# Moving the last chunk's Gram blocks into the first Gram group, with other weight columns and earlier left sums

## The chip, the cores and the metric

The kernel runs on one core of a Trainium2 chip. The metric is the device time of one execution, in microseconds (us). The kernel before takes 1006.29 us, the median of three runs (1004.66 to 1007.55). The changed kernel computes the same function.

## The reference

One layer of a hybrid network runs over 528 frames (16 meta frames and 512 real ones) of width 2048. What has to be computed is, cut to what matters:

```
hn = rmsnorm(h);  P = hn @ w_in                       # 528 x 2048 by 2048 x 8320
r, k, v, g, wl, al = token_shift(P[:, :4224])         # RWKV half: 16 heads of 64
decay = exp(-exp(-softplus(-(w0 + tanh(wl) @ W)) - .5));  a = sigmoid(a0 + al @ A)
kk = normalise(k * k_k);  k = k * (1 + (a - 1) * k_a)
S = S*diag(w) - (S kk)(kk*a)^T + v k^T;  y = S r      # one step per frame
y_a = (groupnorm(y) + bonus) * silu(g)
y_b = B * causal_conv3(C * h) * silu(gc)              # convolution half
out = rmsnorm(h + concat(y_a, y_b) @ w_out)[16:]      # 512 x 2048 by 2048 x 2048
```

## The kernel before, in words

**Precision.** Each large product is made of three products of a 32-bit format that TensorE takes at full pace: high times high, high times low, low times high. For that every operand is split into a high and a low part. Weights arrive by DMA in raw tiles; `split_w` (L134, L135) makes the high part on ACT and the low part on DVE or POOL, into one of six slots of 1152 columns (`slot`). `column(j)` says at which column of the slot the weights of a projection begin: 0, 16 or 80. The high part takes 512 columns from there, and the low part the 512 behind it.

**Projections.** The 65 blocks of 128 columns of w_in are taken in the order of `plan`: low-rank inputs (lora), then k, r, v, g of eight head pairs, mixed with C, h, B, gc of the convolution half. `main` runs one of them: for each of four groups of four k-tiles, `steps` (L328) issues 12 matmuls for each range of frames. k, v and lora have two ranges, of 256 and 272 frames; r, g, C and h of 256 and 258; B and gc one, of 512. For k the ranges are taken in the order (1, 0), for the others (0, 1). The results are in banks of PSUM from the pool `pm`, tag "main", which has four: a projection with two ranges holds two of them, the next one takes the other two. A bank is given back when the instructions that read it have run: `scaled` (L352) on DVE, one piece for the first range and, for k and v, three pieces for the second (256, 2 and 14 columns).

**One stream on TensorE.** TensorE's order is written out by hand. `flow` is a generator that issues one matmul of the projections at a time and charges 0.43 ns for each column; `fill(ns)` takes matmuls from it until their charges add up to `ns`. The recurrence's small steps stand between such fills, so that TensorE always has projection matmuls to do while another engine prepares the next small step. `FW` holds the lengths.

**Preparing a head pair.** `prepare(i)` makes, for head pair i, the decayed keys and queries, and then the Gram blocks of nine chunks of 64 frames. `gram` issues two products per chunk, each shown as two records (L681). First group: after a fill of `FW["gram"]` = 8000 (even pairs) or `FW["gram_b"]` = 13500 (odd pairs) come chunks 0 to 7, into two banks of `pz` (tag "tz") and two of `pi` (tags "misc" and "ser"); `masked` (L691) reads them on DVE, two instructions for each four chunks. After a further fill of `FW["gram2"]` = 5500 comes the second group: chunk 8 into two "tz" banks, the squared norms n2 in two halves (L713, L714; two matmuls each, the second half in the rest of a bank that chunk 8 uses), and zb (L716, L717). ACT copies n2 and zb, and DVE masks chunk 8. `invert`, `load_inverse` and `recur` work further with the results.

**Order on the other engines.** DVE, ACT, POOL and the DMA queues are put in order by a planner ahead of the run: it goes by the order in which the code emits the instructions, moved forward where `ahead()` says so (`masked` and the copies of n2), and takes what is ready by its own times. On the chip each engine then runs its queue strictly in that order.

**Output product.** It is a Strassen-like scheme with seven products per half (`units`: M1, M2, then P5, M7, M3 and Q6 in four groups, P4). `at(u, ...)` attaches work to unit u: splits of weights (`split_unit`, L1215 on ACT, L1216 on DVE), sums of weights (`add`, L1206), sums of the left operand (`sums`, L1118 and L1121 on DVE), their splits (`split_form`, L1173 on ACT, L1174 on DVE), and the closing of products (`onto`, L1224). The four sums of the left operand's second half stand at units 6, 7, 8 and 9.

Of the kernel before, what the change touches and what calls it, by code (L numbers as in the profile page):

```python
# [9 lines left out]
F32 = mybir.dt.float32  # L10
# [8 lines left out]
P = 128  # L19
# [6 lines left out]
NCH = SEQ // CH + 1  # L26
LP = NCH * CH
# [15 lines left out]
FW = dict(  # L43
    evac=34, start=1062, lora=2200, gram=8000, gram_b=13500, gram2=5500, misc=2000, v=2000, vt=1000, solve=24500, solve_first=30000,
    tr=3200, lev=3000, cp=4200, out=1500, begin=19500, p=2900, u=2900, s=5200, last=3700, mix=2600,
)
# [31 lines left out]
def hymba_kernel(ctx: ExitStack, tc: tile.TileContext, xt, xtok, front, w_in, w_out, pv, lup, cst, msk, gf, out):  # L78
# [35 lines left out]

    def column(j):
        what = plan[j][0]
        return {"B": 0, "gc": 0, "v": 80, "g": 80, "h": 80}.get(what, 16)
    stream += [w_out[0, g] for g in range(3)]
    quarters, chain, low = {}, {}, {}
    state = {"next": 0}  # L120
# [5 lines left out]
    def slot_of(q):  # L126
        if q >= 2 * N_IN:
            return slot(f"w{q}", OUT_AT)
        n = q // 2
        return slot(f"w{q}", column(n % 4 if n < 8 else n // 2))  # L130
# [7 lines left out]
    def prefetch(upto):  # L138
        while state["next"] < min(upto, len(stream) if chain else N_IN):
            j = state["next"]  # L140
            raw = chain[j - N_IN] if j >= N_IN else wp.tile([P, 1024], F32, tag="raw", name=f"wr{j}", bufs=3)
            state["dma"] = nc.sync.dma_start(raw, stream[j]).ins
            with tc.high_priority(offset=WEIGHTS):
                for q in range(2):
                    split_w(2 * j + q, raw[:, q * 512 : (q + 1) * 512], nc.gpsimd if q and 10 < j < N_IN else nc.vector)
            state["next"] = j + 1
# [19 lines left out]
    pm = ph1.enter_context(tc.tile_pool(name="pm", bufs=4, space=PSUM))  # L166
    pz = ph1.enter_context(tc.tile_pool(name="pz", bufs=2, space=PSUM))
    pi = ph1.enter_context(tc.tile_pool(name="pi", bufs=1, space=PSUM))
# [5 lines left out]
    def tr(name, dt=F32):  # L174
        return cq.tile([P, LP], dt, tag="tr", name=name, bufs=5)
# [143 lines left out]
    def steps(ps, ranges, k4, q, ks=range(4), rs_=range(2)):  # L319
        hi, lo = quarters[q]  # L320
        for r, (a, b) in enumerate(ranges):
            if r not in rs_:
                continue
            for k in ks:
                kt = 4 * k4 + k
                w = slice(k * P, (k + 1) * P)
                for n, (ww, xx) in enumerate(((hi, xh), (hi, xl), (lo, xh))):
                    nc.tensor.matmul(  # L328
                        ps[r], ww[:, w], xx[:, kt, a:b], start=(kt == 0 and n == 0), stop=(kt == KT - 1 and n == 2)
                    )  # L330
                    yield (b - a) * 0.43

    def banks(ranges, name, pool, tag):
        return [pool.tile([P, b - a], F32, tag=tag, name=f"ps_{name}_{r}") for r, (a, b) in enumerate(ranges)]

    def main(j, ranges, name):
        prefetch(2 * j + 4)
        ps = banks(ranges, name, pm, "main")
        for k4 in range(4):
            if k4 == 1:  # L340
                prefetch(2 * j + 5)
            for r in (1, 0) if name[0] == "k" else range(len(ranges)):
                yield from steps(ps, ranges, k4, 4 * j + k4, rs_=(r,))
        return ps

# [137 lines left out]
    def mains():  # L483
# [34 lines left out]
        for j in range(4, len(plan)):  # L518
            what, i = plan[j]
            rg = FULL if what in ("k", "v") else REAL if what in ("B", "gc") else TAIL  # L520
            ps = yield from main(j, rg, f"{what}{i}")
            if what == "B" and i < 4 or (what, i) == ("gc", 0):
                state["split"] = low[4 * j + 4]
            use(what, i, ps)
# [17 lines left out]
    def step():  # L542
        t = next(flow, None)
        if t is None:
            run_pending(float("inf"))
        else:
            clock[0] += t
            run_pending(clock[0])
        return t

    def fill(ns):
        while ns > 0:
            seen = len(ready)
            t = step()
            if t is None:
                return
            ns -= t
            if len(ready) > seen:
                ns += FW["evac"]
# [5 lines left out]
    def low_rank(i, j, up, w0, name, pad):  # L565
        t = tr(name)
        nc.gpsimd.memset(t[:, META:CH], pad)
        hi, lo = up
        for a, b in ((0, 272), (272, L)):
            z = pz.tile([P, b - a], F32, tag="tz", name=f"{name}_{a}")  # L570
            nc.tensor.matmul(z, hi[:, j], la[:, j, a:b], start=True, stop=False)
            nc.tensor.matmul(z, lo[:, j], la[:, j, a:b], start=False, stop=True)
            with tc.high_priority(offset=AHEAD):
                if a == 0:
                    nc.scalar.activation(t[:, 0:META], z[:, 0:META], AF.Tanh, bias=w0, scale=0.5)
                    nc.scalar.activation(t[:, CH : 5 * CH], z[:, META:272], AF.Tanh, bias=w0, scale=0.5)
                else:
                    nc.scalar.activation(t[:, 5 * CH : LP], z, AF.Tanh, bias=w0, scale=0.5)
            fill(FW["lora"])
        return t  # L580


    def ahead():
        return tc.high_priority(offset=AHEAD)
# [13 lines left out]
    def split(t, name, n):  # L598
        hi = tr(f"{name}_h", F32R)[:, 0:n]
        lo = tr(f"{name}_l", F32R)[:, 0:n]  # L600
        nc.scalar.copy(hi, t)
        nc.vector.tensor_tensor(out=lo, in0=t, in1=hi.bitcast(F32), op=ALU.subtract)
        return hi, lo
# [23 lines left out]
    def prepare(i):  # L627
        p = i % 2
        until("k", i)
        k = got["k", i]  # L630
# [6 lines left out]
        tz = low_rank(i, 0, up, hv[:, 0, i : i + 1], f"tz{i}", -1.0)  # L637
# [26 lines left out]
        r = got["r", i]  # L664
# [8 lines left out]
        nc.scalar.activation(sq, k, AF.Square, scale=col(V_KK, i))  # L673
        sqh, sql = split(sq, f"sq{i}", LP)
        rh, rl = split(r, f"rk{i}", SEQ)
        fill(FW["gram_b" if p else "gram"])

        gt = cq.tile([P, 2, NCH, P], F32, tag=f"gt{p}", name=f"gt{i}")
        def gram(z, c, c0):
            for h, hs, ho in heads:  # L680
                nc.tensor.matmul(  # L681
                    z[h][:, c - c0],
                    bk[hs, c, h : h + 2, :].rearrange("p a s -> p (a s)"),
                    ar[hs, c].rearrange("p a s -> p (a s)"),
                    start=True, stop=True,
                )

        def masked(z, c0, c1):
            with ahead():
                for h in range(2):  # L690
                    nc.vector.tensor_tensor(  # L691
                        out=gt[:, h, c0:c1],
                        in0=z[h],
                        in1=gmask[:, h].unsqueeze(1).to_broadcast([P, c1 - c0, P]),
                        op=ALU.mult,
                    )


        za = [pz.tile([P, 4, P], F32, tag="tz", name=f"g{i}_0_{h}") for h in range(2)]
        zc = [pi.tile([P, 4, P], F32, tag=("misc", "ser")[h], name=f"g{i}_4_{h}") for h in range(2)]  # L700
        for c in range(8):
            gram(za if c < 4 else zc, c, c // 4 * 4)
        masked(za, 0, 4)
        masked(zc, 4, 8)
        fill(FW["gram2"])

        ze = [pz.tile([P, P + 288 * (1 - h)], F32, tag="tz", name=f"g{i}_8_{h}") for h in range(2)]
        gram([z[:, 0:P].unsqueeze(1) for z in ze], 8, 8)
        n2 = tr(f"n2{i}")
        zn = pi.tile([2, 288], F32, tag="misc", name=f"n2_{i}")  # L710
        zs = ((zn, 0, 288), (ze[0][0:2, P : P + 288], 288, LP))
        for z, a, b in zs:
            nc.tensor.matmul(z, ones[:, P : P + 2], sqh[:, a:b], start=True, stop=False)  # L713
            nc.tensor.matmul(z, ones[:, P : P + 2], sql[:, a:b], start=False, stop=True)  # L714
# [3 lines left out]
        with ahead():  # L718
            for z, a, b in zs:
                nc.scalar.copy(n2[0:2, a:b], z)  # L720
            masked([z[:, 0:P].unsqueeze(1) for z in ze], 8, 9)
        nc.scalar.copy(r, zb)
        fill(FW["misc"])

# [90 lines left out]
        v = got["v", i]  # L815
# [246 lines left out]
    for i in range(0, NPAIR, 2):  # L1062
        invert([prepare(i), prepare(i + 1)])
# [155 lines left out]
    def here(t, n):  # L1219
        return xa[t][:, n * 512 : (n + 1) * 512] if n < 2 else xb[n - 2][:, t]  # L1220
# [61 lines left out]
    def at(u, fn, *args):  # L1282
        calls.setdefault(max(u, -1), []).append((fn, args))
# [67 lines left out]
                at(m2 - 2, split_unit, (0, "M2", g), passing(0, 1, 0, g))  # L1351
    for n, f in enumerate(("S1", "S3", "S4", "S5")):
        at((1, 2, 4, 5)[n], split_form, f, 0)
        at(6 + n, sums, 1, (n,))
        at((10, 11, 13, 14)[n], split_form, f, 1)
    for t in range(4):
        at((0, 1, 8, 9)[t], load_xa, t)
# [14 lines left out]
    z = {}  # L1372
    for u, unit in enumerate(units):
        half, prod, g = unit
# [53 lines left out]
    with tc.manual_schedule(engines={mybir.EngineType.DVE, mybir.EngineType.Activation, mybir.EngineType.Pool}):  # L1428
# [16 lines left out]
        for part in range(2):  # L1445
# [7 lines left out]
            h = here(1, 2)[:, cols]  # L1453
# [73 lines left out]
```

## Time and profile before

| | us |
|---|---|
| median of three runs | 1006.29 |
| the profiled execution's own time | 1006.95 |
| its span, first to last instruction | 1005.2 |
| PE busy in the span | 993.7 |
| DVE, ACT, POOL busy | 680.5, 393.2, 264.2 |

The span is the stretch that the trace covers; the time of an execution lies 1.75 us above it here. In rows of groups the columns are the line, the engine, the operation, the result and its operands, the shapes and the count, then the busy time in us and the mean duration of one in ns, then the idle time before them and what ended it. In rows of the timeline they are the start in us from the span's start, the length in us, the engine, the line and the operands, the count of instructions merged into the row, and idle time before it in brackets. Matmuls overlap in the pipeline: two that start 0.11 us apart each last 0.28 us. The pace is therefore read from differences of starts.

### The profile page before, as it was taken

What the parts mean: (1) busy time and instruction counts of PE and PEld (TensorE: products, weight loads), DVE (VectorE), ACT (ScalarE), POOL (GpSimd) and SP (SyncE); (2) the same over time, 40 slices, a digit from 0 to 9 for tenths busy, and PEclk for the clock granted to TensorE, in tenths of its full rate; (3) what the DMA queues carried; (4) which work ended last, traced back from release to release, by engine and by line L of the source; (5) the groups of instructions that cost most, each with busy time, mean ns of one, the idle gap of its engine ahead of it and who ended that gap; (6) DMA issues with size and microseconds to landing.
All of it is one profiled execution on the core that took longest, in us unless ns stands there. A gap on an engine that the chain in (4) does not pass through costs nothing.

```text
span 1005.2 us, 23750 instructions
## 1 busy us (share of the span) xinstructions
PE 993.7 (99%) x9723; PEld 913.6 (91%) x9723; DVE 680.5 (68%) x1313; ACT 393.2 (39%) x729; POOL 264.2 (26%) x286
## 2 busy tenths in 40 slices
PE   9999999999999999999999999999999999999996
PEld 8999998999998999998999998989888898788886
DVE  6777965587775568655668654245554597899996
ACT  7553422344323434323434322223232435545553
POOL 0122323224222323232423222223332333001001
PEclk9999999999999999999999999999999999999998
DMA  9525476446674363864273855978673689688644
GB/s 329 151 83 146 124 191 152 146 119 152 144 185 148 103 169 91 224 159 119 85 171 98 222 143 167 341 243 249 202 226 91 174 270 238 197 267 236 151 105 168
DMA packets 185181, 175.35 MB, mean 174 GB/s; under 512 B 121584, under 2 KB 142832, under 8 KB 184560
## 3 DMA queue, kind: packets, MB, share of 16 engines
q1 hardware_dynamic: 182480, 164.92, 56.4%
q0 software_dynamic: 2304, 8.39, 5.0%
q8 instruction: 76, 1.25, 0.5%
q10 hardware_dynamic: 288, 0.52, 0.1%
q14 instruction: 33, 0.27, 0.1%
HBM read 137.44 MB, written 36.35 MB: 173 GB/s over the span
## 4 chain that ended last, share of the span: by engine, by line
PE 65%; DVE 3%; DMA 1%; ACT 1%; SPq 0%; issue 0%; DVEq 0%; POOL 0%; ACTq 0%
PE ps_gc L328 8%; PE ps_B L328 7%; PE ps_h L328 7%; PE ps_C L328 6%; PE M L1243 5%; PE ps_k L328 5%; PE ps_v L328 5%; PE ps_g L328 5%; PE ps_r L328 5%; PE P L1243 4%; PE Q L1243 2%; PE zy L1010 1%; PE zs L1006 1%; PE g L681 1%; PE rz L954 1%; DVE o L1216 1%
## 5 line engine op out<-in xcount | busy, mean ns | idle before, releaser
L135 POOL TENSOR_TENSOR w<-wr,w 128x512 fp32r<-128x512 f32 x119 | 166.6, 1401 | 366.8 <-ACT w L134 306.2
L134 ACT CAST w<-wr 128x512 fp32r<-128x512 f32 x252 | 153.0, 618 | 280.7 <-PE ps_C L328 46.2
L135 DVE TENSOR_TENSOR w<-wr,w 128x512 fp32r<-128x512 f32 x133 | 95.8, 727 | 102.3 <-ACT w L134 92.2
L328 PE MATMUL ps_k<-xh,w 128*128 128x256 f32 (+1 forms) x512 | 95.8, 285 | 0.1
L328 PE MATMUL ps_r<-xh,w 128*128 128x256 f32 (+1 forms) x512 | 95.1, 281 | 0.0
L328 PE MATMUL ps_v<-xh,w 128*128 128x272 f32 (+1 forms) x512 | 95.0, 283 | 0.0
L328 PE MATMUL ps_h<-xh,w 128*128 128x258 f32 (+1 forms) x512 | 94.1, 282 | 0.0
L328 PE MATMUL ps_C<-xh,w 128*128 128x258 f32 (+1 forms) x512 | 93.2, 281 | 0.0
L328 PE MATMUL ps_g<-xh,w 128*128 128x258 f32 (+1 forms) x512 | 91.9, 281 | 0.0
L328 PE MATMUL ps_B<-xh,w 128*128 128x512 f32 x256 | 83.4, 395 | 0.1
L328 PE MATMUL ps_gc<-xh,w 128*128 128x512 f32 x256 | 81.7, 393 | 0.3 <-DVE w L135 0.3
L328 PEld LDWEIGHTS ps_h<-xh,w 128*128 128x128 f32 x512 | 79.7, 189 | 1.8 <-issue 1.2
L328 PEld LDWEIGHTS ps_k<-xh,w 128*128 128x128 f32 x512 | 80.4, 189 | 0.7 <-DVE w L135 0.3
L328 PEld LDWEIGHTS ps_r<-xh,w 128*128 128x128 f32 x512 | 80.3, 189 | 0.2
L328 PEld LDWEIGHTS ps_v<-xh,w 128*128 128x128 f32 x512 | 80.0, 189 | 0.3
L328 PEld LDWEIGHTS ps_C<-xh,w 128*128 128x128 f32 x512 | 79.7, 189 | 0.6
L328 PEld LDWEIGHTS ps_g<-xh,w 128*128 128x128 f32 x512 | 79.3, 189 | 0.3
L328 PE MATMUL ps_k<-xl,w 128*128 128x272 f32 (+1 forms) x256 | 72.9, 285 | 0.0
L328 PE MATMUL ps_v<-xl,w 128*128 128x256 f32 (+1 forms) x256 | 72.5, 283 | 0.0
L328 PE MATMUL ps_r<-xl,w 128*128 128x256 f32 (+1 forms) x256 | 72.4, 283 | 0.0
L328 PE MATMUL ps_g<-xl,w 128*128 128x256 f32 (+1 forms) x256 | 72.3, 282 | 0.0
L328 PE MATMUL ps_C<-xl,w 128*128 128x256 f32 (+1 forms) x256 | 72.0, 281 | 0.0
(320 smaller groups left out, 2261.9 us busy)
## 6 DMA issues: line engine op xcount, KB each, us to landing
wr<-in_w_in_dram SPq DMA_DIRECT2D x126, 512.0 KB
ct<-opd SPq DMA_DIRECT2D x64, 288.0 KB
wo<-in_w_out_dram SPq DMA_DIRECT2D x21, 512.0 KB
x<-in_w_out_dram POOLq DMA_DIRECT2D x16, 512.0 KB, 5.8
opd<-ar SPq DMA_DIRECT2D x8, 576.0 KB
opd<-gt SPq DMA_DIRECT2D x16, 288.0 KB
opd<-bt SPq DMA_DIRECT2D x64, 64.0 KB
x<-in_w_out_dram SPq DMA_DIRECT2D x8, 512.0 KB
```

Of the source, the lines that this page charges most:

```text
L134: nc.scalar.copy(hi, rq)
L135: low[q] = eng.tensor_tensor(out=lo, in0=rq, in1=hi.bitcast(F32), op=ALU.subtract).ins
L328: nc.tensor.matmul(ps[r], ww[:, w], xx[:, kt, a:b], start=(kt == 0 and n == 0), stop=(kt == KT - 1 and n == 2))
L681: nc.tensor.matmul(z[h][:, c - c0], bk[hs, c, h : h + 2, :].rearrange("p a s -> p (a s)"), ar[hs, c].rearrange("p a s -> p (a s)"), start= ...
L954: nc.tensor.matmul(z[e][ho if e else hs, 0, k], t[hs, o : o + CH], t[hs, O_V : O_V + CH] if part else st[hs, 4 * e + k], start=(part == 0 ...
L1006: nc.tensor.matmul(d[hs, j], w, x[hs], start=(a == 0), stop=(a == b - 1))
L1010: nc.tensor.matmul(d[ho, j], t[hs, o : o + CH], x[hs], start=(a == 0), stop=(a == b - 1))
L1216: nc.vector.tensor_tensor(out=lo, in0=rq, in1=hi.bitcast(F32), op=ALU.subtract)
L1243: nc.tensor.matmul(bank[s], left(prod, jj, m, s), w, start=(jj == 0 and n == 0), stop=(jj == 7 and n == 2))
```

## The change

There are three edits.

First, the columns: lora, k and r weights begin at column 80 of their slots instead of 16, as v, g and h do already; only C stays at 16, and B and gc at 0. The ranges of k are taken in the order (0, 1).

Second, the Gram blocks of chunk 8 are issued with chunks 0 to 7, into two banks of the projections' pool `pm`, and masked right behind the other masks. The fill ahead of the first group is longer by 2000 for pair 0 and by 2500 for pair 1, shorter by 4000 for pair 3; the fill behind it makes up for that, so that the second group stays where it was. In the second group n2 gets one bank of "misc" and one of "tz".

Third, the four left sums of the output stand at units 5, 5, 7 and 9.

```
     def column(j):
-        return {"B": 0, "gc": 0, "v": 80, "g": 80, "h": 80}.get(what, 16)
+        return {"B": 0, "gc": 0, "C": 16}.get(what, 80)
...
-            for r in (1, 0) if name[0] == "k" else range(len(ranges)):
+            for r in range(len(ranges)):
...
-        fill(FW["gram_b" if p else "gram"])
+        shift = {0: 2000, 1: 2500, 3: -4000}.get(i, 0)
+        fill(FW["gram_b" if p else "gram"] + shift)
...
-        for c in range(8):
-            gram(za if c < 4 else zc, c, c // 4 * 4)
+        ze = [pm.tile([P, 1, P], F32, tag="main", name=f"g{i}_8_{h}") for h in range(2)]
+        for c in range(NCH):
+            gram((za, zc, ze)[c // 4], c, c // 4 * 4)
         masked(za, 0, 4)
         masked(zc, 4, 8)
-        fill(FW["gram2"])
-
-        ze = [pz.tile([P, P + 288 * (1 - h)], F32, tag="tz", name=f"g{i}_8_{h}") for h in range(2)]
-        gram([z[:, 0:P].unsqueeze(1) for z in ze], 8, 8)
+        masked(ze, 8, 9)
+        fill(FW["gram2"] - shift)
+
         n2 = tr(f"n2{i}")
-        zn = pi.tile([2, 288], F32, tag="misc", name=f"n2_{i}")
-        zs = ((zn, 0, 288), (ze[0][0:2, P : P + 288], 288, LP))
+        zn = [pool.tile([2, 288], F32, tag=t, name=f"n2_{i}_{t}") for pool, t in ((pi, "misc"), (pz, "tz"))]
+        zs = ((zn[0], 0, 288), (zn[1], 288, LP))
...
-            masked([z[:, 0:P].unsqueeze(1) for z in ze], 8, 9)
...
-        at(6 + n, sums, 1, (n,))
+        at((5, 5, 7, 9)[n], sums, 1, (n,))
```

## The prediction

> **What bounds the kernel now.** I read the page's first part, then the waits of TensorE (PE), then its groups with shapes kept apart, and last the timeline of PE and DVE around the places that the edits touch. The first two say that PE is never short of work:
>
> ```profile
> span 1005.2 us, 23750 instructions
> PE 993.7 (99%) x9723; PEld 913.6 (91%) x9723; DVE 680.5 (68%) x1313; ACT 393.2 (39%) x729; POOL 264.2 (26%) x286
> ```
>
> ```profile
> PE M L1243 <- DVE o L1216: 0.6, 2, 0.4
> PE ps_gc L328 <- DVE w L135: 0.3, 1, 0.3
> ```
>
> The second fence is from the waits of PE (total us, times, longest): its waits for other engines are below a microsecond each. So an edit gains only if PE streams fewer or faster instructions, and it loses whatever wait it puts into PE's row. Both are worked out below against the profiled execution, whose span is 1005.2 us and whose time is 1006.95, that is 0.66 above the median 1006.29. A difference found here is put onto the median.
>
> **Gram blocks of chunk 8: what PE saves.** The two groups of pair 5, in the timeline of PE:
>
> ```profile
> 398.45 2.06 PE L681 MATMUL g<-ar,bk 64*128 64x128 f32 x32
> 400.43 0.38 PE L328 MATMUL ps_g<-xl,w 128*128 128x256 f32 x1
> ...
> 406.33 0.28 PE L328 MATMUL ps_g<-xh,w 128*128 128x256 f32 x1
> 406.54 0.49 PE L681 MATMUL g<-ar,bk 64*128 64x128 f32 x4
> 406.96 0.29 PE L713 MATMUL n<-sq_h,ones 128*2 128x288 f32 x1
> 407.09 0.30 PE L714 MATMUL n<-sq_l,ones 128*2 128x288 f32 x1
> ...
> 407.36 0.30 PE L714 MATMUL g<-sq_l,ones 128*2 128x288 f32 x1
> 407.49 0.40 PE L716 MATMUL zb<-rk_h,ones 128*128 128x512 f32 x1
> ...
> 407.95 0.28 PE L328 MATMUL ps_g<-xh,w 128*128 128x256 f32 x1
> 408.07 0.28 PE L328 MATMUL ps_g<-xl,w 128*128 128x256 f32 x1
> ```
>
> Read the differences of starts. Two projection matmuls stand 0.12 us apart (407.95, 408.07). From the projection at 406.33 to the first Gram record it is 0.21, and four Gram records take until 406.96: 0.63 in all, where an ordinary step would be 0.12. Chunk 8 therefore costs 0.51 us in the second group. In the first group 32 records and the way back take 1.98 us (398.45 to 400.43), 0.06 each, so four more cost 0.24 there. Net 0.27 us per pair, and 8 pairs give 2.2 us less PE time. It is this small because the work itself stays; what goes is one change between tall and half-height tiles.
>
> This supposes that n2 right behind a projection costs no change of its own. Before, n2 always follows Gram records, so the entry isn't shown; the way out is: 407.36 to 407.49 is 0.13 us, as 406.96 to 407.09 inside n2. I bound the entry by 0 (that row) and by 0.09 (0.21 less 0.12, the entry of Gram records), and take 0, since it is the same pair of shapes. At the upper end the saving is 1.5 us.
>
> The Trainium skill, page TensorEngine Tiling (Array Packing), section Key Properties, says that changing the tiling mode drains TensorE, and the page lists 128 rows with 32 columns as a mode of its own. If n2's two columns ran in such a mode, the entry would drain, and the saving would be the 1.5 us of that end in place of 2.2. The way out at 407.49 shows no drain, the entry no run here shows yet.
>
> **What the borrowed banks cost.** First what a wait of PE costs beside the idle time itself, from the one at the output product:
>
> ```profile
> 867.67 0.39 PE L1243 MATMUL M<-o,S 128*128 128x512 f32 x1
> 868.50 5.52 PE L1243 MATMUL M<-o,S 128*128 128x512 f32 x23 [0.43 <-DVE o L1216]
> ```
>
> From 867.67 to 868.50 it is 0.83; an ordinary step of 512 columns is 0.23 (5.52 less the last one's 0.39, over 22 steps), the idle time 0.43, and 0.17 goes into the signal and the refilling of the pipeline.
>
> Chunk 8 now needs two of the four "main" banks while a projection holds the other two. So it waits until the projection before that one has been read out by DVE, and the next projection waits until chunk 8 is masked. Nothing of this exists before. Pair 3 is the case for the first wait. Its Gram group is this:
>
> ```profile
> 256.18 2.06 PE L681 MATMUL g<-ar,bk 64*128 64x128 f32 x32
> ```
>
> It is issued 4000 charges earlier: 36 matmuls of 258 columns at 0.43 ns, 0.12 us apart, 4.3 us. That puts it at 251.9, and chunk 8, 1.9 us into the group, at 253.8, in the middle of g2. The projection before g2 is v3, and DVE reads it out late, at work on pair 2's triangular blocks in between (left out here):
>
> ```profile
> 252.94 0.42 DVE L352 TENSOR_TENSOR pr_v<-ps_v,rs 128x256 f32<-128x256 f32 x1
> ...
> 253.86 0.42 DVE L352 TENSOR_TENSOR pr_v<-ps_v,rs 128x256 f32<-128x256 f32 x1
> ...
> 255.24 0.17 DVE L352 TENSOR_TENSOR pr_v<-ps_v,rs 128x2 f32<-128x2 f32 x1
> ...
> 255.97 0.16 DVE L352 TENSOR_TENSOR pr_v<-ps_v,rs 128x14 f32<-128x14 f32 x1
> ```
>
> The second range's bank is free at 255.97 + 0.16 = 256.13, so chunk 8's second head waits from 253.8: 2.3 us, and 0.2 to start again, 2.5. The queue on DVE isn't fixed, though. The four masks of chunks 0 to 7 are moved forward by the code and are ready between 253.1 and 254.0 in the new place. If the planner sets them ahead of the last piece, it runs four masks later, and PE waits for that too:
>
> ```profile
> 258.97 0.39 DVE L352 TENSOR_TENSOR pr_g<-ps_g,rs 128x256 f32<-128x256 f32 x1
> ...
> 259.87 2.47 DVE L691 TENSOR_TENSOR gt<-g,cs 128x512 f32<-128x512 f32 x4
> 262.26 0.41 DVE L352 TENSOR_TENSOR pr_g<-ps_g,rs 128x256 f32<-128x256 f32 x1
> ```
>
> Four masks hold DVE from 259.87 to 262.26, 2.4 us, which makes the wait 4.9. These masks could have run from 258.2, where the group ended, yet the planner put the read-out of g2's first range and a split ahead of them: DVE runs about 2 us behind the plan there. So the bounds are 0 (v3 read out earlier in a new order) and 4.9; I take 2.5, the one that changes no order in the rows.
>
> The second wait comes where the Gram group stands near the end of a projection: pairs 2, 4 and 6.
>
> ```profile
> 217.81 2.47 DVE L691 TENSOR_TENSOR gt<-g,cs 128x512 f32<-128x512 f32 x4
> 220.21 0.67 DVE L135 TENSOR_TENSOR w<-wr,w 128x512 fp32r<-128x512 f32 x1
> ...
> 356.09 2.48 DVE L691 TENSOR_TENSOR gt<-g,cs 128x512 f32<-128x512 f32 x4
> 358.48 0.75 DVE L352 TENSOR_TENSOR pr_v<-ps_v,rs 128x256 f32<-128x256 f32 x2
> ...
> 511.72 0.29 DVE L691 TENSOR_TENSOR gt<-g,cs 128x128 f32<-128x128 f32 x1
> ```
>
> ```profile
> 219.97 0.28 PE L328 MATMUL ps_r<-xh,w 128*128 128x256 f32 x1
> ...
> 358.40 0.29 PE L328 MATMUL ps_k<-xh,w 128*128 128x272 f32 x1
> ```
>
> In pair 4 the four masks end at 358.48; chunk 8's first mask, 0.29 like the one at 511.72, ends at 358.77. k5 would start at 358.40 + 0.24 = 358.64, so it waits 0.13 and 0.17, 0.3. Pair 6 is issued by the same charges as pair 4: another 0.3. In pair 2, 220.21 + 0.29 = 220.50 against 219.97 + 0.24: 0.3 and 0.17. Together 1.1 us; bounds 0 (masks planned earlier) and 3 (one L135 of 0.67 in front of each first mask). The second range's bank follows 0.2 later, while the first range runs 12 matmuls, 1.4 us, so it is hidden. In the other four pairs the Gram group stands early in a projection, far from its end, and I count nothing; pair 5 has the least room on the other side, with v5's read-out about done when chunk 8 comes.
>
> On the other queues: the 16 masks of chunk 8 are as many as before, but they run ahead of read-outs and L135 splits, which come 0.4 us later each time. This is hidden, since the next projection uses chunk 8's banks; without that cover it is 0.4 us times eight, 3 us. ACT's copies of n2 and zb stay, and SP's stores of gt are tied to the second group, which stays; POOL gets nothing.
>
> **Columns and the order of k.** Groups with shapes kept apart, PE:
>
> ```profile
> L328 PE MATMUL ps_r<-xh,w 128*128 128x256 f32 x256 | 51.8, 280 | 0.0
> L328 PE MATMUL ps_k<-xh,w 128*128 128x256 f32 x256 | 51.4, 282 | 0.0
> L328 PE MATMUL ps_v<-xh,w 128*128 128x256 f32 x256 | 50.5, 280 | 0.0
> L328 PE MATMUL ps_C<-xh,w 128*128 128x256 f32 x256 | 50.3, 279 | 0.0
> L328 PE MATMUL ps_g<-xh,w 128*128 128x256 f32 x256 | 50.1, 278 | 0.0
> ```
>
> At column 16 stand k (282), r (280) and C (279), at column 80 v (280) and g (278). Within one column the means differ by as much as between the two, so the column isn't what sorts them; k and v, which are slowest, are those whose other range is 272. If k went to C's 279 and r to g's 278, 384 first-range matmuls each would save 1.2 + 0.8 = 2.0 us, and the loss has the same bound with the signs turned. I take 0. The new order of k gives its first bank to DVE sooner and moves no matmul.
>
> **Left sums.** DVE at the first block:
>
> ```profile
> 856.46 1.22 DVE L1174 TENSOR_TENSOR S<-mix,S 128x1024 fp32r<-128x1024 f32 x1
> 860.74 0.69 DVE L1216 TENSOR_TENSOR o<-wo,o 128x512 fp32r<-128x512 f32 x1 [3.07 <-ACT o L1215]
> ...
> 863.15 1.22 DVE L1118 TENSOR_TENSOR mix<-mix 128x1024 f32<-128x1024 f32 x1
> 864.28 1.28 DVE L1216 TENSOR_TENSOR o<-x,o 128x512 fp32r<-128x512 f32 x2
> ```
>
> DVE idles 3.07 us, the number in brackets, ahead of 860.74 and is then behind, so that PE loses 0.6 at 868.50 (0.83 against a step of 0.23, above). The second sum takes DVE 1.13 us (863.15 to 864.28). Put into the idle stretch it would take up to 1.1 us out of PE's waits. But unit 5 also holds the split at 856.46, which runs before the idle stretch now; the sum is emitted ahead of it, so they may simply change places, and the split then delays the second weight split of M2 by 0.6, of which PE sees 0.5, given back at 868.50. Bounds: 1.1 less and 0.5 more. I take 0, the change of places. The third sum goes ahead of M3's splits, which PE needs only after M7's 12 matmuls.
>
> **Sum.** -2.2 + 2.5 + 1.1 + 0 + 0 = +1.4, so 1008.35 for the profiled execution and 1007.7 for the median: no change that a measurement tells (0.3%, 3.0 us here). Own range of this case 1005 to 1009.
>
> **Rivals.**
> - Slower: the four masks overtake v3's last piece. Pair 3 then waits 4.9 and the sum is +3.8, 1010.1. For it: the masks are moved forward and ready at 253.1, the last piece starts at 255.97. Against: DVE's lag behind its plan, seen at 259.87. It decides from a wait of 4.1 on in pair 3.
> - Faster: v3 is read out before 253.8 and the sum does land in the idle stretch: -2.2 - 1.1 + 0.3 = -3.0, 1003.3; half of the columns' bound on top gives 1002.3. For it: the idle 3.07 and DVE's freedom to reorder. Against: three pieces of v3 would have to move up 2 us on an engine without a gap.
> - The tile change stays at n2's entry: +0.7 on each case, 1008.4 with the forecast. Against it stands the 0.13 at 407.49. Chance 0.15, spread over the others, since alone it decides nothing.
>
> **Numbers.** Forecast 0.37, slower rival 0.34, faster 0.29. So faster by over 0.3% 0.29, within 0.37, slower 0.34. The range reaches from the faster case with half the columns to the slower with the second wait 1.0 larger: 1002.3 to 1011.1.
>
> **What would show it.** L681 as x36 in one group and none ahead of L713; the step into L713 0.12 (right) or 0.2 (the drain). A wait of PE for DVE L352 at about 254, 2.3 or 4.7 us idle, and for L691 at 220, 358 and 508. Means of k's and r's 256-column rows unchanged. DVE's L1118 ahead of or behind 860, and the step at 868.50. The forecast is wrong if pair 3 doesn't wait, or if masks stand ahead of v3's pieces.

## The result and the profile after

The changed kernel takes 1003.43 us, the median of 17 runs (1001.15 to 1004.87), against 1005.04 us (1004.03 to 1007.65) for 17 runs of the kernel before run beside it. The ratio is 0.9979, with a 95% interval of 0.9971 to 0.9987: 2.1 us faster by the ratio (1.6 by the medians), where 1.4 us slower was forecast. The profiled execution of the changed kernel took 1003.54 us, close to its median. Line numbers behind the edit are one higher in it: the Gram products are L682, the masks L692, n2 L714 and L715, zb L717 and L718.

The span, the busy times and the waits of PE (total us, times, longest), from the page and the waits of the changed kernel:

```profile
span 1001.7 us, 23771 instructions
PE 989.9 (99%) x9723; PEld 913.8 (91%) x9723; DVE 687.3 (69%) x1313; ACT 393.5 (39%) x729; POOL 272.3 (27%) x286
PE ps_g L328 <- DVE gt L692: 0.2, 1, 0.2
```

The two waits that the prediction quoted for the kernel before, at gc for L135 and at the output product for L1216, are both gone, and one new wait, for the masks, stands in their place. Pair 5's groups, in the timeline of PE:

```profile
396.34 2.28 PE L682 MATMUL g<-ar,bk 64*128 64x128 f32 x36
398.55 0.39 PE L328 MATMUL ps_g<-xl,w 128*128 128x256 f32 x1
...
404.44 0.28 PE L328 MATMUL ps_g<-xh,w 128*128 128x256 f32 x1
404.56 0.30 PE L714 MATMUL n_misc<-sq_h,ones 128*2 128x288 f32 x1
404.69 0.30 PE L715 MATMUL n_misc<-sq_l,ones 128*2 128x288 f32 x1
...
405.09 0.40 PE L717 MATMUL zb<-rk_h,ones 128*128 128x512 f32 x1
```

The first group takes 2.21 us until the next projection (396.34 to 398.55) in place of 1.98, so four more records cost 0.23. The step into n2 is 0.12 (404.44 to 404.56), an ordinary step. The Gram part of the change behaves as forecast.

The two traces are not on one clock: what an edit gains early in the kernel moves all that follows, and the start itself varies. So instants of two traces are compared here by their distance from a matmul that both have. For pair 3 that is v3's first one, in the kernel before and then in the changed one:

```profile
233.10 0.28 PE L328 MATMUL ps_v<-xh,w 128*128 128x256 f32 x1
```

```profile
230.51 0.28 PE L328 MATMUL ps_v<-xh,w 128*128 128x256 f32 x1
```

Pair 3 in the changed kernel, first PE, then DVE, then SP's queue:

```profile
249.37 2.85 PE L682 MATMUL g<-ar,bk 64*128 64x128 f32 x36
257.48 0.36 PE L328 MATMUL ps_g<-xh,w 128*128 128x256 f32 x1 [0.21 <-DVE gt L692]
```

```profile
242.90 1.05 DVE L774 TENSOR_TENSOR prod<-d,y 72x512 f32<-72x512 f32 x1
...
248.86 0.68 DVE L789 TENSOR_REDUCE y<-prod 72x64 f32<-72x512 f32 x1
...
250.72 0.89 DVE L352 TENSOR_TENSOR pr_v<-ps_v,rs 128x256 f32<-128x256 f32 x4
```

```profile
217.67 1.38 SPq L621 DMA_DIRECT2D sg<-gt  x2
```

The group lasts 2.85 us, where it lasts 2.28 without a wait (pair 5, above), so chunk 8 costs 0.57 us of waiting, not 2.5. The reason stands in DVE's rows: v3 is read out in one go by 251.61, 21.1 us after v3's first matmul, where in the kernel before it took until 256.13, 23.0 us after it. Of the 4.5 us between the two instants, 2.6 are the shift of the whole trace and 1.9 are a real advance. Pair 2's triangular blocks, whose last step (L774 of 72x512 and what follows) ran among v3's pieces from 18.9 us after v3's start on (251.97), now run from 12.4 us after it and end at 249.54, ahead of v3's first piece. Their input, the Gram scratch sg, is also stored earlier: 5.4 us after the first record of pair 2's Gram group (212.25), against 9.1 us (from 214.51) in the kernel before, whose SP queue shows

```profile
223.62 0.58 SPq L621 DMA_DIRECT2D sg<-gt  x1
...
224.78 0.58 SPq L621 DMA_DIRECT2D sg<-gt  x1
```

since the store of gt has to wait for chunk 8's mask. Whether these stores are why v3 is read out sooner is taken up with the late stores below.

In pair 4 the second wait doesn't exist (DVE, then PE):

```profile
354.24 2.87 DVE L692 TENSOR_TENSOR gt<-g,cs 128x512 f32<-128x512 f32 x6
```

```profile
356.80 0.28 PE L328 MATMUL ps_k<-xh,w 128*128 128x256 f32 x1
```

The masks start 2.56 us ahead of k5 (356.80 less 354.24), as the prediction had it (358.64 less 356.09 is 2.55). What differs is the order: in DVE's queue chunk 8's first mask is fourth of the six, not fifth. It starts at 356.03 and ends at 356.31, 0.49 us before k5.

A ruler for the experiments: the start of v0's first matmul and that of C3's bound a stretch that holds all eight Gram preparations. In the kernel before:

```profile
54.28 0.28 PE L328 MATMUL ps_v<-xh,w 128*128 128x256 f32 x1
...
571.31 0.28 PE L328 MATMUL ps_C<-xh,w 128*128 128x256 f32 x1
```

That is 517.03 us, and in two more profiled executions of the same kernel (below) 517.08 and 517.07. So this stretch repeats within 0.05 us, while the whole time spreads over more than 3 us. In the changed kernel it is

```profile
53.56 0.28 PE L328 MATMUL ps_v<-xh,w 128*128 128x256 f32 x1
...
568.31 0.28 PE L328 MATMUL ps_C<-xh,w 128*128 128x256 f32 x1
```

514.75: 2.28 us less, about as much as the ratio gives for the whole. All of the runs, cut at the first matmuls of the projections named (us; gc0 to r2 holds no Gram group, v3 to C1 holds pair 3's; "output" is from the first output product to the last start on PE; lengths are taken from unrounded starts):

```
kernel                       v0-gc0 gc0-r2  r2-v3  v3-C1   C1-C3   v0-C3  output  ratio
before                       100.25  26.12  52.45  38.55  299.65  517.03  154.52
before, 2nd execution        100.31  26.11  52.43  38.55  299.67  517.08  152.52
before, 3rd execution        100.31  26.09  52.45  38.55  299.67  517.07  153.02
changed                       99.76  25.07  52.12  39.33  298.47  514.74  152.52  0.9979
Gram alone                    99.75  25.06  52.17  39.65  298.55  515.18  152.52  0.9980
left sums alone              100.26  26.08  52.43  38.55  299.67  517.00  152.52  1.0001
columns alone                100.29  26.16  52.56  38.57  299.54  517.12  155.28  0.9996
late stores                   99.78  26.66  52.12  39.47  298.59  516.62  154.38  1.0001
same copies, not held         99.71  25.07  52.10  39.37  298.59  514.84  152.52  0.9980
pair 3 without shift          99.71  25.07  52.10  39.44  298.47  514.79  152.70  0.9979
pair 3 shifted by -6500       99.71  25.07  52.12  41.50  298.49  516.89  152.53  1.0015
chunk 8 first in pair 3       99.76  25.07  52.11  38.49  298.49  513.92  153.29  0.9966
```

What lies outside these columns varies too: in three executions of the kernel before v0 starts at 53.4 to 54.3 us, and from C3 to the first output product it is 271.4 to 272.2.

### The profile page after: what moved, and what is told of

Read it like the earlier page. It is cut to its first block, busy times and chain, and to the rows that moved or that the text cites. A ratio compares the mean times of both kernels' runs of the same rounds, so it can differ in the third digit from the quotient of the medians.

```text
span 1001.7 us, 23771 instructions
## 1 busy us (share of the span) xinstructions
PE 989.9 (99%) x9723; PEld 913.8 (91%) x9723; DVE 687.3 (69%) x1313; ACT 393.5 (39%) x729; POOL 272.3 (27%) x286
## 4 chain that ended last, share of the span: by engine, by line
PE 68%; DVE 1%; DMA 1%; issue 0%; SPq 0%; ACT 0%; DVEq 0%; POOL 0%
PE ps_gc L328 8%; PE M L1243 8%; PE ps_B L328 7%; PE ps_h L328 7%; PE ps_C L328 6%; PE ps_k L328 5%; PE ps_v L328 5%; PE ps_g L328 5%; PE ps_r L328 5%; PE P L1243 4%; PE Q L1243 2%; PE zy L1010 1%; PE zs L1006 1%; PE rz L954 1%; PE g L682 1%; PE end L1450 1%
## 5 line engine op out<-in xcount | busy, mean ns | idle before, releaser
L135 POOL TENSOR_TENSOR w<-wr,w 128x512 fp32r<-128x512 f32 x119 | 174.3, 1466 | 349.7 <-ACT w L134 290.5
L134 ACT CAST w<-wr 128x512 fp32r<-128x512 f32 x252 | 152.8, 618 | 281.9 <-PE ps_k L328 45.4
L135 DVE TENSOR_TENSOR w<-wr,w 128x512 fp32r<-128x512 f32 x133 | 98.7, 747 | 105.5 <-ACT w L134 105.2
L328 PE MATMUL ps_k<-xl,w 128*128 128x256 f32 (+1 forms) x256 | 72.9, 285 | 0.0
```

The costliest lines, as they stand in the source:

```text
L134: nc.scalar.copy(hi, rq)
L135: low[q] = eng.tensor_tensor(out=lo, in0=rq, in1=hi.bitcast(F32), op=ALU.subtract).ins
L328: nc.tensor.matmul(ps[r], ww[:, w], xx[:, kt, a:b], start=(kt == 0 and n == 0), stop=(kt == KT - 1 and n == 2))
```

## The experiments

### The three edits alone

The Gram edit alone is the change without these:

```
-        return {"B": 0, "gc": 0, "v": 80, "g": 80, "h": 80}.get(what, 16)
+        return {"B": 0, "gc": 0, "C": 16}.get(what, 80)
-            for r in (1, 0) if name[0] == "k" else range(len(ranges)):
+            for r in range(len(ranges)):
-        at(6 + n, sums, 1, (n,))
+        at((5, 5, 7, 9)[n], sums, 1, (n,))
```

> Only the second edit: chunk 8 in the first Gram group on projection banks, with its shifts; columns, order of k and sums as before. Theory: the tile change saves 2.2 us over eight pairs, and of the waits of the forecast only pair 3's two stand, 0.6 in the group and 0.4 behind it (as in the trace of the changed kernel), so 1.2 us less than before. In the trace: 36 Gram records in the first group, v3 read out before 252, the output phase 162.4 us as before with its two waits for L1216. Rival (the forecast's own sum): the waits eat the saving, 0 to 1.4 us more than before, and what was gained comes from the other edits.

Measured: 1003.51 us, ratio 0.998 (0.9971 to 0.9988), by the ratio all of the change's gain. The stretch is 1.85 us shorter, 0.43 less than with all three edits; 0.32 of that lies from v3 to C1, where pair 3's two waits cost more (1.10 longer than in the kernel before, against 0.78). One part of the expectation fell: the output phase was 152.52 us, without the waits for L1216, though the sums stand where they stood.

The last pair of lines alone:

> Only the third edit: left sums at units 5, 5, 7, 9. Theory: the second sum moves into DVE's idle stretch of 3.07 us, the waits of PE for L1216 at the output product (0.6 us idle, some 1.0 with the restarts) go, and the output phase is 1 us shorter: 1.0 us less than before. Rival (the forecast): the sum and the split of unit 5 change places, the waits stay, 0.0 with bounds of 1.1 less and 0.5 more. A second rival: the 2.0 us that the output phase is shorter in the two profiled executions are all due to the sums.

Measured: 1005.26 us, ratio 1.0001 (0.9993 to 1.001). The waits for L1216 are absent in its profile, and yet nothing is gained: the forecast's 0 stands, and the theory behind the 1.0 fell. Why is shown further down.

The first two pairs of lines alone:

> Only the first edit: lora, k and r weights at column 80, k's ranges in the order (0, 1). Theory: the column doesn't set the pace, so 0.0 within 0.3 us; k's and r's 256-column means stay at 280 to 282 ns with the order of k turned. Rival: the columns save 0.5 to 2.0 us, seen as a smaller step between matmuls of k and r.

Measured: 1004.98 us, ratio 0.9996 (0.9987 to 1.0006). k and r by groups with shapes kept apart:

```profile
L328 PE MATMUL ps_r<-xh,w 128*128 128x256 f32 x256 | 52.0, 280 | 0.0
L328 PE MATMUL ps_k<-xh,w 128*128 128x256 f32 x256 | 51.1, 281 | 0.1
```

280 and 281 ns after 280 and 282: the column doesn't set the pace. Alone this edit leaves the stretch nearly as it was (517.12). So the gain is the Gram edit's, but for the 0.43 us above, which the columns or the order of k add only together with it; which of the two, and how, wasn't tested.

### What the earlier masks and stores do

The changed kernel, with chunk 8 masked into a tile of its own that ACT copies into gt behind the copies of n2:

```
-        masked(ze, 8, 9)
+        g8 = cq.tile([P, 2, P], F32, tag="g8", name=f"g8_{i}")
+        with ahead():
+            for h in range(2):
+                nc.vector.tensor_tensor(out=g8[:, h], in0=ze[h][:, 0], in1=gmask[:, h], op=ALU.mult)
...
-                nc.scalar.copy(n2[0:2, a:b], z)
+                last = nc.scalar.copy(n2[0:2, a:b], z).ins
+            with tc.issue_after(last):
+                nc.scalar.copy(gt[:, :, 8], g8)
```

> The changed kernel, but chunk 8's masks write a tile of their own, and ACT copies it into gt only behind the copies of n2, so that the stores of gt can't start earlier than they did in the kernel before. Theory: the early stores (217.7 against 223.6 us) are what moved pair 2's triangular blocks up on DVE and v3's read-out from 256 to 251.6. With the stores late again v3's last piece runs at about 255, PE waits 2 us or more in pair 3's first Gram group in place of 0.57, and the time is 1.5 to 2.5 us above the changed kernel, so 0 to 0.5 us under the kernel before. Rival: the planner reads v3 out early because chunk 8 needs its bank; then v3 is read out at 251 again, the wait stays at 0.6, and the time is that of the changed kernel, 2 us under the one before.

Measured: 1005.84 us, ratio 1.0001 (0.9991 to 1.001). The gain is gone, as expected, but not where it was expected. DVE at v3 (L779 and L794 are L774 and L789 here):

```profile
251.81 0.14 DVE L352 TENSOR_TENSOR pr_v<-ps_v,rs 128x2 f32<-128x2 f32 x1
251.92 1.04 DVE L779 TENSOR_TENSOR prod<-d,y 72x512 f32<-72x512 f32 x1
252.89 0.15 DVE L352 TENSOR_TENSOR pr_v<-ps_v,rs 128x14 f32<-128x14 f32 x1
```

v3 starts at 232.36 here, so its last piece, which ends at 253.04, ends 20.7 us after v3's first matmul. One of pair 2's blocks stands ahead of that piece, and still the read-out is over sooner than in the changed kernel (21.1); pair 3 hardly waits for it (its group is 2.43 us long; g3 waits 0.81 us for L134 behind it). The stores are late in this trace, as meant: sg is stored from 223.9 on, 8.5 us ahead of v3's first matmul, against 9.5 in the kernel before and 12.8 in the changed one. So v3's earlier read-out doesn't need the early stores, and this part of the theory fell. The rival's account of v3, that the planner reads it out because chunk 8 needs its bank, fits, but no run tests it; and with the columns alone, where chunk 8 asks for no such bank, v3's read-out also ended sooner than in the kernel before, 21.9 us after v3's first matmul. Why the planner moved it stays open.

What came back is another wait, between gc0 and r2, where the stretch is 26.66 us against 25.07. This is DVE and PE there in the kernel before, then with late stores, then DVE in the changed kernel, where PE doesn't wait. gc0's first matmul is at 154.53, 153.57 and 153.32.

```profile
155.77 0.69 DVE L789 TENSOR_REDUCE y<-prod 72x64 f32<-72x512 f32 x1
156.36 0.16 DVE L352 TENSOR_TENSOR hh<-ps_h,rs 128x2 f32<-128x2 f32 x1
158.69 1.54 DVE L429 SCALAR_TENSOR_TENSOR cv<-u,pvt,cv 128x512 f32<-128x512 f32 x2 [2.16 <-ACT cv L427]
160.14 2.38 DVE L135 TENSOR_TENSOR w<-wr,w 128x512 fp32r<-128x512 f32 x2
```

```profile
160.88 0.73 PE L328 MATMUL ps_gc<-xh,w 128*128 128x512 f32 x2 [0.27 <-DVE w L135]
```

```profile
158.30 0.67 DVE L794 TENSOR_REDUCE y<-prod 72x64 f32<-72x512 f32 x1
158.90 0.73 DVE L429 SCALAR_TENSOR_TENSOR cv<-u,pvt,cv 128x512 f32<-128x512 f32 x1
159.56 1.28 DVE L135 TENSOR_TENSOR w<-wr,w 128x512 fp32r<-128x512 f32 x2
```

```profile
160.29 0.73 PE L328 MATMUL ps_gc<-xh,w 128*128 128x512 f32 x2 [0.63 <-DVE w L135]
```

```profile
150.95 0.68 DVE L789 TENSOR_REDUCE y<-prod 72x64 f32<-72x512 f32 x1
...
153.53 0.49 DVE L352 TENSOR_TENSOR hh<-ps_h,rs 128x256 f32<-128x256 f32 x2 [1.02 <-PE ps_h L328]
156.18 0.75 DVE L429 SCALAR_TENSOR_TENSOR cv<-u,pvt,cv 128x512 f32<-128x512 f32 x1 [2.16 <-ACT cv L427]
156.85 0.69 DVE L135 TENSOR_TENSOR w<-wr,w 128x512 fp32r<-128x512 f32 x1
```

Pair 1's triangular blocks end 1.9 us after gc0's first matmul in the kernel before (156.46), 5.4 us after it with late stores (158.97), and 1.7 us ahead of it in the changed kernel (151.63). The low parts of gc0's weights (L135) begin 5.6, 6.0 and 3.5 us after it (160.14, 159.56 and 156.85). In the kernel before the blocks are some way ahead of them, and the delay is passed on: the blocks stand among the pieces of h0's read-out, which ends 2.0 us after gc0's first matmul (156.52) and not 0.7 (154.02 in the changed kernel). From it POOL and ACT make cv, DVE idles 2.16 us for that in both kernels, and then two L429 run ahead of L135, in the changed kernel one. With late stores two L429 and a block between them run ahead of it. Where L135 is late, gc0's matmuls stand and start again. That is 1.05 us between gc0 and r2 (26.12 to 25.07), which no term of the forecast held.

It isn't that pair 1's data come late on the chip. With late stores its blocks d are loaded at 134.79, 18.8 us ahead of gc0's first matmul, in the kernel before at 136.41, 18.1 us ahead of it; and DVE idles ahead of h0's read-out:

```profile
134.79 0.31 SPq L621 DMA_DIRECT2D d<-sg  x1
```

```profile
152.33 0.42 DVE L352 TENSOR_TENSOR hh<-ps_h,rs 128x256 f32<-128x256 f32 x1 [3.95 <-PE ps_h L328]
152.67 0.20 DVE L794 TENSOR_REDUCE y<-prod 72x16 f32<-72x64 f32 x1
```

The rest of the blocks stands behind that read-out in DVE's queue and waits 3.95 us with it. What counts is the order that the planner wrote.

The control has the same copies on ACT, without the line that holds them:

```
-                last = nc.scalar.copy(n2[0:2, a:b], z).ins
-            with tc.issue_after(last):
-                nc.scalar.copy(gt[:, :, 8], g8)
+                nc.scalar.copy(n2[0:2, a:b], z)
+            nc.scalar.copy(gt[:, :, 8], g8)
```

> As the run with the late stores, with the same ACT copies of chunk 8 into gt, but these are not held behind the copies of n2. Theory: what the late stores lost (1.9 us between the starts of v0 and of C3, of which 1.6 lie between gc0 and r2, where PE waits for L135 again) was lost by the place of the triangular blocks on DVE and not by the added ACT copies. So here PE doesn't wait at gc0, the stretch from v0 to C3 is 2.0 to 2.3 us shorter than in the kernel before, and the time is that of the changed kernel, ratio 0.998. Rival: the added copies and tile cost it, and the time is again that of the kernel before, ratio 1.000.

Measured: 1003.35 us, ratio 0.998 (0.9971 to 0.9989); gc0 to r2 is 25.07 again and the stretch 2.19 shorter. The added copies cost nothing. What costs is the hold: with it the planner, which has gt complete later, puts the triangular blocks later in DVE's queue.

### Pair 3's two waits

One number is changed in each of the next two:

```
-        shift = {0: 2000, 1: 2500, 3: -4000}.get(i, 0)
+        shift = {0: 2000, 1: 2500}.get(i, 0)
```

> The changed kernel with no shift for pair 3: its first Gram group 36 matmuls or 4.3 us later, at 253.7. Theory: v3's bank is long free by then, so the first wait (0.57) is gone; the second one grows, since chunk 8's first mask now runs fourth in a row that can start at 256.0 and ends near 258.9, while g3 wants to start at 256.5: 2.4 us idle and 0.2 to start again in place of 0.37. Net 1.6 us above the changed kernel, ratio to the kernel before 0.9995. Rival: the second wait is hidden, as in pairs 2, 4 and 6, and the kernel is 0.6 to 0.9 us faster than the changed one, ratio 0.997.

Measured: 1003.24 us, ratio 0.9979 (0.9971 to 0.9988), neither of the two. PE, then DVE:

```profile
254.08 2.28 PE L682 MATMUL g<-ar,bk 64*128 64x128 f32 x36
...
259.46 0.38 PE L328 MATMUL ps_g<-xh,w 128*128 128x258 f32 x1 [0.92 <-DVE gt L692]
```

```profile
255.74 0.41 DVE L352 TENSOR_TENSOR pr_g<-ps_g,rs 128x256 f32<-128x256 f32 x1
...
258.56 1.64 DVE L692 TENSOR_TENSOR gt<-g,cs 128x512 f32<-128x512 f32 x4
```

The first wait is gone (2.28). The second is 0.92, and it stands at the range of 258 columns, g3's second one: its first range started 2.5 us earlier, ahead of chunk 8's masks, so it didn't use one of their banks. DVE had begun to read out g2's first range at 255.74, and that is the only other bank that came free, so g3 must have taken it. I had taken for granted that the next projection gets both of chunk 8's banks; here it gets only one of them.

With a shift of -6500:

```
+        shift = {0: 2000, 1: 2500, 3: -6500}.get(i, 0)
```

> The changed kernel with a shift of -6500 in place of -4000 for pair 3: the first Gram group 22 matmuls or 2.7 us earlier, at 246.7, and chunk 8 at 248.5. Theory (the mechanism of the forecast, with v3's read-out as it now stands, 250.7 to 251.6): PE waits for v3's banks 2.7 us longer, 3.1 in place of 0.57 with the restart, and none for the masks at g3, so 2.2 to 2.7 us above the changed kernel, ratio 1.0003. Rival: DVE reads v3 out earlier when PE asks for the bank earlier; then the wait stays under 1 us and the time stays that of the changed kernel.

Measured: 1006.94 us, ratio 1.0015 (1.0006 to 1.0024), slower than the kernel before.

```profile
247.72 2.06 PE L682 MATMUL g<-ar,bk 64*128 64x128 f32 x32
252.10 1.02 PE L682 MATMUL g<-ar,bk 64*128 64x128 f32 x4 [2.32 <-DVE pr_v L352]
```

```profile
251.62 0.90 DVE L352 TENSOR_TENSOR pr_v<-ps_v,rs 128x256 f32<-128x256 f32 x4
```

Here is the wait of the forecast: 2.32 us for v3's pieces, and v3 to C1 is 2.17 us longer than in the changed kernel, at the lower end of the 2.2 to 2.7 expected. v3 starts at 231.45 in this trace and is read out by 252.52, 21.1 us after its first matmul, as in the changed kernel; DVE doesn't hurry for PE. The stretch is 0.14 us shorter than before, though, and the ratio says 1.5 longer. The interval's lower end leaves at least 0.6 us that the stretch doesn't show. One thing goes along with it: the granted clock of TensorE was 0.995 to 0.997 in ten of this kernel's eleven executions (mean of all 0.9961), where the 27 of the kernel before beside them have 0.997 to 0.999 (mean 0.9978). If the time went with the clock, that difference of 0.0017 would be 1.7 us, an estimate. The profiled execution is the eleventh, at 0.998, and with 1005.33 us the fastest; so no trace shows where the clock was lower, and the cause stays open. That this kernel is slower than the one before can't be put down to the wait.

At last a version for which both waits are taken away: in pair 3 chunk 8 goes first, when v3's banks are just free, and is masked first.

```
-        shift = {0: 2000, 1: 2500, 3: -4000}.get(i, 0)
+        shift = {0: 2000, 1: 2500, 3: -2000}.get(i, 0)
...
-        for c in range(NCH):
+        for c in (8, *range(8)) if i == 3 else range(NCH):
```

> A version meant to beat both: the changed kernel, where pair 3 alone issues chunk 8 ahead of chunks 0 to 7 and has a shift of -2000, so that chunk 8 comes at 251.5, when v3's banks are free, and its masks come first on DVE. Theory: both waits of pair 3 (0.57 and 0.37) go, 0.9 us less than the changed kernel, ratio to the kernel before 0.997. Rival: the later masks of chunks 0 to 7 delay the second group or a weight split, and the gain is lost again, ratio 0.998.

Measured: 1001.94 us, ratio 0.9966 (0.9953 to 0.9978), 3.4 us faster than the kernel before and the lowest of all, though its interval overlaps that of the changed kernel. The stretch decides: it is 0.82 us shorter than in the changed kernel (513.92), all of it from v3 to C1 (38.49); of the two waits 0.24 is left (a group of 2.52 us, from 251.94).

### Where the output phase's 2 us come from

Two more profiled executions of the kernel before, nothing changed:

> The kernel before, unchanged, for a second profiled execution. Theory: the 2.0 us by which the output phase is longer in the profile of before (162.5 against 160.5 us from the first output product to the end) belong to that execution, since the phase was also short with the sums in their old place and long with them in the new one; ACT's idle time ahead of the split at 860 (3.74 us, for the weight's DMA) varies from run to run. So here that idle time may be anything between 0.4 and 4.5 us and the phase 160.4 to 163.3 us, while the wait of PE for L135 in gc0 (0.2 to 0.3) and the distance from gc0 to r2 (26.1 us) stay as they were. Rival: the output phase is 162.5 us again with about 3.7 us idle on ACT; then it belongs to the kernel before.

> The kernel before, unchanged, a third profiled execution. Expectations as for the second: the stretch from gc0 to r2 26.1 us by both, the output phase between 160.4 and 163.3 us by the theory, and 162.5 by the rival.

Measured: 1005.56 and 1004.61 us. From gc0 to r2 both have 26.1 us, and the wait for L135. Their output phases are 2.0 and 1.5 us shorter than in the first profile. The splits of M2's weights on ACT show what differs. The first two rows are of the kernel before, in its first and second profiled execution; then columns alone (sums in the old place), then late stores (sums in the new place, L1220 for L1215):

```profile
860.09 1.14 ACT L1215 CAST o<-wo 128x512 fp32r<-128x512 f32 x2 [3.74 <-DMA wo<-in_w_out_dram]
```

```profile
857.79 1.14 ACT L1215 CAST o<-wo 128x512 fp32r<-128x512 f32 x2 [0.86 <-DMA wo<-in_w_out_dram]
```

```profile
861.11 1.14 ACT L1215 CAST o<-wo 128x512 fp32r<-128x512 f32 x2 [4.49 <-DMA wo<-in_w_out_dram]
```

```profile
859.62 1.14 ACT L1220 CAST o<-wo 128x512 fp32r<-128x512 f32 x2 [3.59 <-DMA wo<-in_w_out_dram]
```

ACT waits for a weight's DMA, 0.3 to 4.5 us over the twelve profiles. The phase is 152.5 us (once 153.0) where it waits up to 1 us, 152.7 and 153.3 where it waits 1.9 and 2.5 (pair 3 without shift, chunk 8 first), and 154.4 to 155.3 where it waits 3.6 or more, whether the sums stand in their old place or the new one. The longest, columns alone, was profiled in the slowest of that kernel's executions (1008.40 us). The idle stretch of 3.07 us on DVE that the prediction read goes with ACT's wait: it is 0.18 us in the second execution of the same kernel and absent in the third. The 2.0 us by which the output phase is shorter in the first profile of after are of this kind, too.

## Why the prediction was wrong

- **Gram saving, -2.2: right.** Seven of the eight pairs lie outside v3 to C1. From the table, changed less before: v0 to gc0 (pairs 0 and 1) -0.5, r2 to v3 (pair 2) -0.3, C1 to C3 (pairs 4 to 7) -1.2: 0.29 per pair for 0.27 forecast, 2.3 over eight. n2's entry is an ordinary step, 0.12. The Trainium skill, page TensorEngine Tiling (Array Packing), section Key Properties, says that a change of tiling mode drains TensorE. The trace agrees for the entry into the Gram tiles, 0.21 us against 0.12 for an ordinary step, and n2's entry shows no such cost.
- **First wait, +2.5: this step failed.** "I take 2.5, the one that changes no order in the rows." It measured 0.57, because the order did change: v3's read-out ended 21.1 us after v3's first matmul and not 23.0, no longer with pair 2's triangular blocks among its pieces. The price of waiting was about right. In the run at -6500 chunk 8's second head would have come at about 249.7 and its bank came free at 252.52; with 0.2 to start again that is 3.0 us, and v3 to C1 is 3.2 us longer than 38.26 (38.55 less the pair's 0.29). That 0.57 lies in the lower part of the range that I gave (0 to 4.9) shows no more than that the range was wide; the choice inside it was wrong, since the row that I kept fixed stood behind work that the planner was free to move. Why it moved stays open: the late stores show that earlier stores aren't needed for it.
- **Second wait, +1.1: failed too.** In pairs 2, 4 and 6 nothing is waited for. The 0.24 us by which the next projection comes later was in the sum; the place of chunk 8's first mask, fourth of six and not behind the four others, was wrong. A wait for the masks came in pair 3 instead, 0.37 us (v3 to C1 is 0.78 longer; with the pair's 0.29 saved, both waits cost 1.07, of which 0.57 is the first and 0.13 is not placed). And which banks the next projection takes isn't fixed.
- **Left out: -1.05.** The wait of gc for L135 was quoted as 0.3 us and then not asked about. It goes, and its restart and the shorter waits behind it go too, since h0 is read out and L135 runs earlier once pair 1's blocks are out of the way. That the blocks' place in the queue does it is shown by the late stores against the control. Without it the change would have gained about 1.2 us. (That the waits of PE are all below a microsecond was misread, too: its page of waits has one of 1.4 us for L184 at the start, which no edit touches.)
- **Columns, 0, and sums, 0: right,** by 0.9996 and 1.0001. The reason given for the sums, that a split and a sum change places, is what the new order shows (the second sum, L1118, at 855.01, and the split, L1174, at 857.08); but the wait that they were weighed against varies from run to run.

The sum with the measured terms: -2.3 + 0.57 + 0.4 - 1.05 = -2.4, against -2.28 in the stretch and -2.1 by the ratio. The forecast's +1.4 differs by 2.6 for the waits and by 1.05 for the one left out. Of the rivals, the faster one, given 0.29, had the right event in part: v3 was read out earlier, though not quite ahead of chunk 8. Its other half, a gain from the sums, didn't come, and it didn't hold the 1.05 at gc0; so that its 1003.3 is close to the median of 1003.43 is luck.

## What to carry to other kernels

When work moves forward, follow its results to the engine that reads them next: chunk 8's masks, done earlier, let the planner move a chain of small instructions up in DVE's queue, and that took away a wait in another projection, at gc0, which the edit doesn't touch. An order that a planner makes isn't fixed by the rows of the old profile, so a wait that rests on such a row needs a chance for each order, and the small waits already in the profile belong among the terms. Instants of two traces are compared from a common event, not from the start: of 4.5 us at v3's read-out only 1.9 were its own. And before a stall is entered as something to win, look whether it is there in a second execution.

## What the runs showed of the hardware

In the output phase the kernel before keeps its DMA engines busy for 0.98 of the time from 840 to 860 us, at 246 GB/s:

```profile
840.00:860.00 20.00, 20.00 (x90) 16.56 (x89) 14.63 (x19) 12.39 (x19) 1.82 (x3) 1.00 0.98 246
```

There ACT's wait for one weight was 3.74, 0.86 and 0.41 us in three executions of the same kernel, and PE's phase 154.52, 152.52 and 153.02 us. From v0 to C3, 517 us, the same three executions agree within 0.05 us, so that single profiles show differences of 0.3 us there; in the output phase they don't.
